# A two-layer hybrid decoder trunk on one core: the low part of every second weight unit made by an accumulating transfer

## The chip, the cores and the metric

The kernel runs on 1 core of one Trainium2 chip. The metric is the device time of one execution in microseconds. Three runs of the kernel before gave 2230.68, 2228.06 and 2229.37 us, a median of 2229.37 us.

## The reference

The program is a float32 trunk of two layers over 512 tokens of width 1024. Each layer has an adaLN-modulated RMS norm, a mixer with three parallel branches (retention, RG-LRU, mLSTM), then a second norm and a squared-ReLU MLP of width 4096. Cut to what matters:

```python
for l in range(2):
    mod = silu(c) @ w_ada[l] + b_ada[l]          # 6 x 1024 columns
    sh1, sc1, g1, sh2, sc2, g2 = split(mod, 6)
    h = rms_norm(x, norm_mix[l]) * (1 + sc1) + sh1
    proj = h @ w_in[l]                           # 1024 -> 8192
    ret, lru, mls = the three branches of proj
    merged = sum(sigmoid(gate_b) * (branch_b @ w_br_b[l]))
    x = x + g1 * (merged @ w_out[l])
    h = rms_norm(x, norm_mlp[l]) * (1 + sc2) + sh2
    x = x + g2 * (square(relu(h @ w_ff1[l])) @ w_ff2[l])
return rms_norm(x, final_norm)
```

Nearly all the arithmetic is in products with weights, and all of it is asked for in float32.

## The kernel before, in words

Activations lie with features on partitions and the 512 tokens along the free axis. A weight matrix is cut into units: a unit is 128x1024 float32 (512 KB), the weights of 128 output features for all 1024 input features. There are 352 units, 176 a layer, counted from 0 in the order of use (`plan_units`, L100).

TensorE multiplies in fp32r, a shortened float32. So every operand is split in two fp32r parts, a high part that ScalarE makes by a copy (L96) and a low part, the operand minus the high part (L97), and each product is three matmuls: high times high (L184), high times low (L185), low weights times high (L186). A unit is 8 such groups of three, 24 matmuls over 512 columns (`project`, L188, and `unit_products`, L198). In the retention's values the tokens are the stationary side, and the three matmuls stand on L923 to L925.

The weight stream is written out by hand. `next_w` (L154) moves the count of used units on and calls `w_ahead` (L141), which emits loads of raw units on SP's queue so that three are ahead of use, and splits so that two units are ready beyond the one in use. Three buffers hold raw units (`raw`), three the high parts (`wh`), three the low parts (`wl`). So the split of unit n can start when TensorE has finished unit n-3, and from then two units' products run before unit n is wanted. `split_next` (L149) makes one split: high part on ScalarE, low part on VectorE, or on GpSimd for the first five units (`split_engine`).

Three places use the buffers otherwise. `update_x` (L203) takes its last three units at once and runs them first over one half of the tokens, then over the other, so their buffers come free late. `first_units` (L230), which follows each inner norm, takes the next three at once in the same way. `ret_values` (L910) takes two at once. `update_x` followed by `first_units` comes three times: from mixer to MLP in both layers, and from the MLP of layer 0 to the mixer of layer 1.

The modulation is computed beside the products. `ada_unit` (L380) loads a 512 KB piece of `w_ada` into a `raw` buffer and VectorE multiplies it with the condition in two instructions. 80 such pieces are emitted one after each unit (`step`, L168) in the first two `merge` stages of layer 0 and in its MLP, so there weight units and modulation pieces share the three `raw` buffers and SP's queue.

The framework that compiles the kernel puts the instructions of each engine in order, chooses the buffers and writes the semaphores. GpSimd (POOL) has 155 small instructions and issues no transfers.

Of the kernel before, what the change touches and what calls it, by code (L numbers as in the profile page):

```python
# [9 lines left out]
F32 = mybir.dt.float32  # L10
# [3 lines left out]
ALU = mybir.AluOpType  # L14
# [11 lines left out]
# column offsets in the packed parameter array of a layer  # L26
# [5 lines left out]
# column offsets in the packed constants  # L32
# [3 lines left out]
# order in which the columns of the modulation are computed: (which of the six, k tile)  # L36
# [7 lines left out]
# causal score blocks: key tile -> (first query column, columns, offset in the packed scores)  # L44
# [3 lines left out]
# order of the mLSTM's input (m) and output gate (o) tiles, in the first layer and in the others  # L48
M_ORDER = ("mmmmmoommmoo", "mmmommommmoo")

# input projection tiles (of 128 columns) by part
# [3 lines left out]
class Trunk:  # L55
# [38 lines left out]
    def split(self, hi, lo, src, eng=None):  # L94
        """hi + lo == src exactly; both are float32r."""
        self.act(hi, src, AF.Copy)  # L96
        self.tt(lo, src, hi.bitcast(F32), ALU.subtract, eng)  # L97

# [50 lines left out]
    def split_next(self, wh, wl):  # L149
        self.split(wh, wl, self.raw.pop(self.n_split), self.split_engine)  # L150
        self.parts[self.n_split] = (wh, wl)
        self.n_split += 1

    def next_w(self, count=1):  # L154
        """The next weight units, with the ones after them on their way."""
        self.n_used += count
        self.w_ahead(3, 2)
        return self.take_w(count)
# [5 lines left out]
    def later(self, units, f):  # L164
        """Emit f after that many more units of products."""
# [22 lines left out]
    def project(self, hs):  # L188
        """The next unit's 128 output features (partitions) for all tokens."""
# [13 lines left out]
    def update_x(self, hs, gate, follow):  # L203
        """x += gate * (hs times the next eight units), and what follow makes of the new x.

        The last three units go through the first half of the tokens and then through the second,
        so that the norm of the first half passes behind the products of the second.
        follow(0) and follow(1) return what is to be emitted for TensorE a unit later."""
# [21 lines left out]
    def first_units(self, hs_half, late):  # L230
        """The next three units, for the first half of the tokens and then for the second.

        hs_half(h) yields the split tokens of a half, k tile by k tile; late() is emitted early on."""
# [16 lines left out]
    def total(self, ps, src, first=True, last=True):  # L250
        """Sum over partitions, on every partition, of a split src."""
# [5 lines left out]
    def setup(self):  # L257
# [29 lines left out]
        # silu of the condition  # L287
# [11 lines left out]
    def small_params(self):  # L299
        """Halved biases and 2 softplus(-lambda) of every layer, one column per feature tile."""  # L300
# [16 lines left out]
        # e = exp(-|lam|): powers of two split off, a polynomial for the rest  # L317
# [14 lines left out]
        # log(1 + e) = 2 atanh(e / (2 + e))  # L332
# [9 lines left out]
        # softplus(-lam) = max(-lam, 0) + 2 q  # L342
# [5 lines left out]
    def rotary_angles(self):  # L348
        """Position times frequency, brought into [-pi, pi]."""
# [30 lines left out]
    def ada_unit(self, l, c, i):  # L380
        """Products of two k tiles with a chunk of 512 modulation columns, summed over the k tiles."""
# [15 lines left out]
    def ada_load(self, l, c, tag="qk"):  # L397
        """The weights of a chunk of 512 modulation columns, a tile for each k tile."""
# [7 lines left out]
    def ada_mixed(self, raws, on_pe):  # L406
        """The sums of a chunk on every partition, the first on_pe k tiles on TensorE and the others on VectorE."""
# [17 lines left out]
    def ada_columns(self, l, i, ps):  # L425
        """Four column tiles of the modulation from their values along the free axis."""
# [28 lines left out]
    def square_sum(self, k, cols=ALL):  # L455
        """Running sum of squares of x[0..6]; x[7] is left apart."""
# [4 lines left out]
        if 0 < k < KT - 1:  # L461
            acc = self.sq_tiles[0][:, cols]
            self.tt(acc, acc, sq, ALU.add)
            if k == KT - 2:
                # has the table of the root loaded before the root is waited for
                self.act(sq[:, :1], sq[:, :1], AF.Sqrt)

    def row_scale(self, cols=ALL):
        """1 / sqrt(mean of squares + eps) per token, on every partition."""
# [22 lines left out]
    def modulated(self, l, second, late):  # L492
        """The normed and modulated tokens, split, and the products of the next three units."""
# [9 lines left out]
    def first_modulated(self):  # L503
        """As modulated, for the first layer, with the modulation itself and the first units' products."""
        count = 3
        # VectorE has the modulation to do
# [17 lines left out]
        # two more units, kept where nothing else is yet  # L524
# [25 lines left out]
    def gate_weights(self, l):  # L550
        """w_if applied after the block-diagonal q, k, v maps: one [1024, 8] map per input, split."""
# [12 lines left out]
        # the blocks of Wq Wk^T, of which the scores are made  # L564
# [6 lines left out]
        # the silu branch arrives doubled  # L571
# [8 lines left out]
    def conv(self, ps, cw, cb, j):  # L580
        """Causal depthwise convolution of a projected tile along the tokens."""
# [7 lines left out]
    def m_first(self, l, j, ps):  # L589
        """Convolution of one tile of the mLSTM input, and the input split for its gates."""  # L590
# [8 lines left out]
    def m_second(self, pg, first):  # L599
        """Twice the silu of the convolution, split for the gates."""  # L600
# [19 lines left out]
    def m_rows(self, l, pg):  # L620
        """Stabiliser rows of the four heads from the gate pre-activations."""
# [23 lines left out]
        # running maximum, split over partitions 0..3 and 32..35  # L645
# [6 lines left out]
        # 4 eps exp(-2 (F + max))  # L652
# [530 lines left out]
def lay_out(v):  # L1183
# [12 lines left out]
    o = {}  # L1196
# [71 lines left out]
```

## Time and profile before

| | |
|---|---|
| median of three runs | 2229.37 us |
| span of the profiled execution, first to last instruction | 2226.5 us |
| TensorE (PE) busy | 2180.9 us, 98% of the span |
| VectorE (DVE) busy | 1387.4 us, 62% |
| ScalarE (ACT) busy | 1037.8 us, 47% |
| GpSimd (POOL) busy | 171.9 us, 8% |
| moved by DMA | 248.93 MB, 112 GB/s on average |

The profiled execution has no time of its own beside its span; the median of the runs is 2.8 us above that span, which is taken as what lies around it. PE is the row of matmuls and PEld the row of weight loads that overlap them. Matmuls are pipelined: one shows as some 0.39 us and the next starts 0.23 us later, so busy time alone doesn't tell whether TensorE is fed; start times do.

### The profile page before, as it was taken

Reading aid. Unit: us, or ns where it says so; the run is one execution under the profiler, and the core shown is the slowest. Engines: PE = TensorE matmul, PEld = TensorE weight load, DVE = VectorE, ACT = ScalarE, POOL = GpSimd, SP = SyncE. Lnnn points to the kernel's source line nnn. Section 1 sums busy time; section 2 is a strip of 40 time slices with the busy share of each in tenths; the row PEclk is TensorE's granted clock in tenths of the full one; section 3 lists DMA queues with packets and bytes.
Section 4 is the critical chain, followed back from the end, with each engine's and each line's share of the span. In section 5 each row is a group of like instructions: output and inputs, shape, how many; then the busy total and the mean of one; then the engine's idle time right before and its main releaser. Section 6 shows DMA issues by size and latency. Waiting matters only on the chain.

```text
span 2226.5 us, 26615 instructions
## 1 busy us (share of the span) xinstructions
PE 2180.9 (98%) x10534; PEld 1817.5 (82%) x10534; DVE 1387.4 (62%) x1867; ACT 1037.8 (47%) x1474; POOL 171.9 (8%) x155
## 2 busy tenths in 40 slices
PE   5999999999999999999999999999999999999998
PEld 3778888888878888888897888888887889888887
DVE  7879766766774576666477872557547556333335
ACT  3566335562583353342446652455528525342342
POOL 2322001002100000000001210000111000000000
PEclk9999999999999999999999999999999999999999
DMA  8211552226423246656322123232322332322322
GB/s 288 74 46 46 171 176 81 96 91 211 129 74 114 86 150 194 188 189 190 125 83 89 34 72 102 84 97 78 107 95 81 95 100 88 96 94 99 100 95 67
DMA packets 75375, 248.93 MB, mean 112 GB/s; under 512 B 8561, under 2 KB 12273, under 8 KB 75249
## 3 DMA queue, kind: packets, MB, share of 16 engines
q1 hardware_dynamic: 75248, 247.23, 35.1%
q8 instruction: 82, 1.34, 0.2%
q14 instruction: 45, 0.36, 0.0%
HBM read 245.10 MB, written 2.10 MB: 111 GB/s over the span
## 4 chain that ended last, share of the span: by engine, by line
PE 85%; DVE 7%; ACT 5%; DMA 2%; issue 1%; SPq 0%; POOL 0%; DVEq 0%; ACTq 0%
PE acc L185 26%; PE acc L186 26%; PE acc L184 26%; PE acc L925 1%; PE acc L924 1%; PE acc L923 1%; ACT t L80 1%; DVE t L83 1%; DVE wl L86 1%; ACT L80 1%; ACT wh L80 1%; DVE qk L1033 1%; DMA big<-in_w_ada 1%; DVE sl L86 0%; PE acc L254 0%
## 5 line engine op out<-in xcount | busy, mean ns | idle before, releaser
L80 ACT ACTIVATE wh<-raw 128x1024 fp32r<-128x1024 f32 x350 | 370.4, 1059 | 834.4 <-PE acc L185 760.4
L185 PE MATMUL acc<-hl,wh 128*128 128x512 f32 (+1 forms) x1720 | 657.1, 383 | 1.5 <-DVE hl L83 1.5
L184 PE MATMUL acc<-hh,wh 128*128 128x512 f32 (+1 forms) x1720 | 655.6, 383 | 2.5 <-ACT hh L80 2.2
L186 PE MATMUL acc<-hh,wl 128*128 128x512 f32 (+1 forms) x1720 | 655.9, 382 | 0.9 <-DVE wl L86 0.9
L86 DVE TENSOR_TENSOR wl<-raw,wh 128x1024 fp32r<-128x1024 f32 x347 | 433.6, 1250 | 317.9 <-ACT wh L80 313.2
L184 PEld LDWEIGHTS acc<-hh,wh 128*128 128x128 f32 x1720 | 323.6, 189 | 71.1 <-ACT hh L80 4.0
L185 PEld LDWEIGHTS acc<-hl,wh 128*128 128x128 f32 x1720 | 324.7, 189 | 64.5 <-DVE hl L83 2.7
L186 PEld LDWEIGHTS acc<-hh,wl 128*128 128x128 f32 x1720 | 324.7, 189 | 64.5 <-DVE wl L86 1.5
L184 PE MATMUL acc<-big,wh 128*128 128x512 f32 (+1 forms) x944 | 357.5, 379 | 0.0
L186 PE MATMUL acc<-big,wl 128*128 128x512 f32 (+1 forms) x944 | 357.4, 379 | 0.0
L185 PE MATMUL acc<-big,wh 128*128 128x512 f32 (+1 forms) x944 | 357.3, 378 | 0.0
L186 PEld LDWEIGHTS acc<-big,wl 128*128 128x128 f32 x944 | 177.6, 188 | 33.7 <-DVE wl L86 0.7
L185 PEld LDWEIGHTS acc<-big,wh 128*128 128x128 f32 x944 | 177.6, 188 | 33.7 <-DVE big L86 0.3
L184 PEld LDWEIGHTS acc<-big,wh 128*128 128x128 f32 x944 | 177.6, 188 | 33.3
L83 DVE SCALAR_TENSOR_TENSOR ada<-raw,cond,ada 128x512 f32<-128x512 f32 x140 | 104.7, 748 | 61.2 <-DMA raw<-in_w_ada 59.5
L83 DVE SCALAR_TENSOR_TENSOR x<-acc,mod,x 128x512 f32<-128x512 f32 (+1 forms) x70 | 49.1, 702 | 126.1 <-PE acc L186 125.9
L80 ACT ACT_TABLE_LOAD x72 | 92.4, 1283 | 6.8 <-DVE t L83 4.9
L80 ACT ACTIVATE t<-t 128x512 f32<-128x512 f32 (+3 forms) x120 | 72.0, 600 | 19.6 <-DVE t L86 8.0
L924 PE MATMUL acc<-wl,hh 128*128 128x256 f32 x256 | 72.4, 283 | 0.0
L925 PE MATMUL acc<-wh,hl 128*128 128x256 f32 x256 | 72.4, 283 | 0.0
L923 PE MATMUL acc<-wh,hh 128*128 128x256 f32 x256 | 72.4, 283 | 0.0
L83 DVE SCALAR_TENSOR_TENSOR t<-acc,par,t 128x511 f32<-128x511 f32 (+2 forms) x96 | 70.1, 739 | 3.3 <-ACT t L80 3.0
(260 smaller groups left out, 2581.7 us busy)
## 6 DMA issues: line engine op xcount, KB each, us to landing
raw<-in_w_in SPq DMA_DIRECT2D x160, 512.0 KB, 3.5
raw<-in_w_ff SPq DMA_DIRECT2D x128, 512.0 KB, 3.5
raw<-in_w_ada SPq DMA_DIRECT2D x80, 512.0 KB, 3.5
raw<-in_w_br SPq DMA_DIRECT2D x48, 512.0 KB, 3.6
raw<-in_w_out SPq DMA_DIRECT2D x16, 512.0 KB, 3.5
qk<-in_w_ada SPq DMA_DIRECT2D x16, 256.0 KB, 5.3
big<-in_w_ada SPq DMA_DIRECT2D x16, 256.0 KB, 6.0
bd<-in_decay SPq DMA_DIRECT2D x8, 320.0 KB, 2.9
```

The costliest lines, as they stand in the source:

```text
L80: self.nc.scalar.activation(out, in_, f, **kw)
L83: self.nc.vector.scalar_tensor_tensor(out, a, s, b, op0=op0, op1=op1)
L86: (eng or self.nc.vector).tensor_tensor(out, a, b, op=op)
L184: mm(ps, lhsT=wh, rhs=xh, start=first, stop=False)
L185: mm(ps, lhsT=wh, rhs=xl, start=False, stop=False)
L186: mm(ps, lhsT=wl, rhs=xh, start=False, stop=last)
L923: mm(dst, lhsT=hh[:, tok], rhs=wh, start=kt == 0, stop=False)
L924: mm(dst, lhsT=hh[:, tok], rhs=wl, start=False, stop=False)
L925: mm(dst, lhsT=hl[:, tok], rhs=wh, start=False, stop=kt == KT - 1)
L1033: self.nc.vector.tensor_tensor_scan(ix, a, w, 0.0, op0=ALU.mult, op1=ALU.add)
```

## The change

In `split_next`, a unit with an odd number (and not among the first five, which have a `split_engine`) gets its low part in two steps: ScalarE writes the negated high part into `wl`, and a transfer issued from POOL's queue adds the raw unit onto it. All other units are split as before. The buffer that the framework keeps for descriptors of POOL's transfers grows from 1024 to 2048 bytes a partition.

```diff
     def split_next(self, wh, wl):
-        self.split(wh, wl, self.raw.pop(self.n_split), self.split_engine)
+        raw = self.raw.pop(self.n_split)
+        if self.n_split % 2 and self.split_engine is None:
+
+            self.act(wh, raw, AF.Copy)
+            self.act(wl, wh.bitcast(F32), AF.Copy, scale=-1.0)
+            self.nc.gpsimd.dma_start(wl.bitcast(F32), raw, accum_op=ALU.add)
+        else:
+            self.split(wh, wl, raw, self.split_engine)
         self.parts[self.n_split] = (wh, wl)
         self.n_split += 1
...
-    nc = bacc.Bacc("TRN2", target_bir_lowering=False, num_devices=1, dynamic_dma_scratch_size=1024)
+    nc = bacc.Bacc("TRN2", target_bir_lowering=False, num_devices=1, dynamic_dma_scratch_size=2048)
```

The rest of the diff removes comments and docstrings.

## Rows read from the trace of the kernel before

**Rows 1.** The page: busy time of the engines, and TensorE's in 40 slices.

```profile
PE 2180.9 (98%) x10534; PEld 1817.5 (82%) x10534; DVE 1387.4 (62%) x1867; ACT 1037.8 (47%) x1474; POOL 171.9 (8%) x155
PE   5999999999999999999999999999999999999998
```

**Rows 2.** The page's groups: the two halves of a split, busy and mean ns.

```profile
L80 ACT ACTIVATE wh<-raw 128x1024 fp32r<-128x1024 f32 x350 | 370.4, 1059 | 834.4 <-PE acc L185 760.4
L86 DVE TENSOR_TENSOR wl<-raw,wh 128x1024 fp32r<-128x1024 f32 x347 | 433.6, 1250 | 317.9 <-ACT wh L80 313.2
```

**Rows 3.** Waits of TensorE's weight loads that VectorE ended: total us, times, longest.

```profile
PEld acc L185 <- DVE xs L86: 5.2, 8, 0.9
PEld acc L185 <- DVE sl L86: 2.5, 4, 0.8
PEld acc L186 <- DVE wl L86: 2.2, 5, 0.5
```

**Rows 4.** Timeline, an ordinary unit of layer 1's MLP: start us, us, instruction [idle before].

```profile
1902.81 1.06 ACT L80 ACTIVATE wh<-raw 128x1024 fp32r<-128x1024 f32 x1 [2.56 <-PE acc L185]
1903.91 1.23 DVE L86 TENSOR_TENSOR wl<-raw,wh 128x1024 fp32r<-128x1024 f32 x1 [2.93 <-ACT wh L80]
...
1914.17 0.39 PE L186 MATMUL acc<-big,wl 128*128 128x512 f32 x1
```

**Rows 5.** Timeline, three odd units around layer 1's inner norm: split start, first low-part matmul.

```profile
1843.50 1.06 ACT L80 ACTIVATE wh<-raw 128x1024 fp32r<-128x1024 f32 x1 [4.00 <-PE acc L185]
1849.42 0.28 PE L186 MATMUL acc<-mg,wl 128*128 128x256 f32 x1
...
1858.69 1.06 ACT L80 ACTIVATE wh<-raw 128x1024 fp32r<-128x1024 f32 x1 [1.98 <-PE acc L185]
1862.48 0.28 PE L186 MATMUL acc<-hh,wl 128*128 128x256 f32 x1
...
1879.33 2.01 ACT L80 ACTIVATE wh<-raw 128x1024 fp32r<-128x1024 f32 x2 [2.75 <-PE acc L185]
1881.95 0.40 PE L186 MATMUL acc<-hh,wl 128*128 128x512 f32 x1
```

**Rows 6.** Timeline, the same pair for two odd units of the RG-LRU's part, layer 0.

```profile
488.67 1.05 ACT L80 ACTIVATE wh<-raw 128x1024 fp32r<-128x1024 f32 x1
494.83 0.39 PE L186 MATMUL acc<-hh,wl 128*128 128x512 f32 x1
...
666.35 1.06 ACT L80 ACTIVATE wh<-raw 128x1024 fp32r<-128x1024 f32 x1
673.27 0.39 PE L186 MATMUL acc<-hh,wl 128*128 128x512 f32 x1
```

**Rows 7.** DMA issues: queue, operation, count, KB each, median us from issue to landing.

```profile
raw<-in_w_ff SPq DMA_DIRECT2D x128, 512.0 KB, 3.5
raw<-in_w_ada SPq DMA_DIRECT2D x80, 512.0 KB, 3.5
...
gcols<-in_gcols SPq DMA_DIRECT2D x1, 8.0 KB, 1.6
```

**Rows 8.** Timeline of layer 0's MLP: two odd units' splits and the loads between.

```profile
897.61 1.06 ACT L80 ACTIVATE wh<-raw 128x1024 fp32r<-128x1024 f32 x1 [2.56 <-PE acc L185]
898.91 1.21 DVE L86 TENSOR_TENSOR wl<-raw,wh 128x1024 fp32r<-128x1024 f32 x1
900.16 0.33 SPq L138 DMA_DIRECT2D raw<-in_w_ff  x1
902.87 0.33 SPq L138 DMA_DIRECT2D raw<-in_w_ada  x1
...
909.35 1.04 ACT L80 ACTIVATE wh<-raw 128x1024 fp32r<-128x1024 f32 x1
```

**Rows 9.** Timeline of POOL: the same addition twice, in the second merge.

```profile
501.67 3.48 POOL L86 TENSOR_TENSOR mg<-mg,t 128x512 f32<-128x512 f32 x1 [5.86 <-DVE t L83]
512.36 1.30 POOL L86 TENSOR_TENSOR mg<-mg,t 128x512 f32<-128x512 f32 x1 [7.22 <-DVE t L83]
```

**Rows 10.** Stretches around the mLSTM's gate rows: us, busy us (instructions), granted clock, DMA share.

```profile
116.00:121.40 5.40, 3.23 (x12) 0.80 (x10) 3.09 (x4) 3.79 (x7) 1.73 (x2) 1.00 0.00 0
121.40:124.90 3.50, 3.50 (x8) 2.32 (x8) 1.26 (x3) 2.26 (x4) 0.00 (x0) 0.51 0.53 154
```

## The prediction

> **What bounds the kernel now.** I read the page's busy times first, then the waits of TensorE, then the timeline of single units. TensorE is at 9 tenths or more in every slice but the first and the last, 98% overall, and VectorE at 62% [rows 1]. So VectorE's load is not what sets the time. What it could give back is what TensorE waits for it: the longest such waits of the weight loads sum to 5.2 + 2.5 + 2.2 = 9.9 us in the whole run, and of these the subtraction that the change takes away accounts for 2.2 [rows 3]. That is the ceiling of a gain: some 10 us. The loss has no such ceiling, because the low part of a weight unit lies on a chain that ends at a matmul.
>
> That chain is read in the timeline. In an ordinary unit ScalarE starts the high part at 1902.81, as TensorE frees the buffer; VectorE's subtraction runs from 1903.91 to 1905.14; the first matmul that reads the low part starts at 1914.17 [rows 4]. I call the time from the first to the last of these the lead: 11.36 us, of which the split now takes 2.3 and 9.0 are spare. The lead is two units of products, and it's this that covers the change. It is not the same everywhere. Around a norm three units hold all three buffers to the end, and the odd units there have leads of 5.92, 3.79 and 2.62 us [rows 5]. In the RG-LRU's part ScalarE comes late to two odd units: 6.16 and 6.92 us [rows 6].
>
> **The change part by part.** It touches the odd units from 5 to 351, 174 of them.
>
> *Removed:* 174 subtractions of 1.25 us, 217 us of VectorE [rows 2]. As it isn't the bound, this is worth between nothing and the 9.9 us above; I take 3, the subtraction's own 2.2 and a little of the rest.
>
> *Added on ScalarE:* 174 passes of 1.06 us, 184 us [rows 2]. ScalarE is at 47% and mostly waits for TensorE before a split, so next to long leads this costs nothing; without that cover each would cost 1.06. Where it falls ahead of the normed tokens' pass at the three norms I count it: 3 us.
>
> *Added on POOL and the DMA engines:* 174 transfers of 512 KB. POOL's instruction waits for ScalarE's second pass, and POOL's own additions and masks queue behind it; POOL is at 8%, so I price that at nothing, at most a POOL instruction (1.3 to 3.5 us [rows 9]) for the few that a scan waits for. No row shows a transfer from POOL's queue, nor one that adds. The nearest are the plain loads: 512 KB lands 3.5 us after issue, 8 KB after 1.6 [rows 7]. So 1.6 is fixed and 1.9 is data. An adding transfer must read two operands for each byte written; I take the data part twice, 1.6 + 3.8 = 5.4 us. The bounds are 3.5 (an addition that costs nothing) and 7.3 (data part three times: two reads and a write), and above that whatever POOL's start adds. I take 5.4 as the plain load is the nearest row and the second operand is certain.
>
> The Trainium skill, "DMA: Bandwidth & Descriptors", section on the anatomy of a DMA on the gpsimd path, fits 2.0 us plus bytes at 436 GB/s for a transfer issued there, an estimate of 3.2 us here. By it the sum below would come to about 2238 us, the cheap case among the rivals. It is a fit for copies, and no run shown so far has one.
>
> So the chain of an odd unit becomes 1.06 + 1.06 + some 0.1 of hand-overs + 5.4 = 7.6 us, in place of 2.3. Against an ordinary lead of 11.36 it stays hidden, with 3.7 to spare. Against the short leads TensorE waits:
> - at each norm 7.6 - 5.9, 7.6 - 3.8 and 7.6 - 2.6: 1.7 + 3.8 + 5.0 = 10.5; three times: 31.5 us;
> - the last odd unit, like the first of these: 1.7;
> - two units at 6.16 and two at 6.92, one of each in either layer: 2 x 1.4 + 2 x 0.7 = 4.2.
>
> Together 37.4 us. These waits don't overlap, as each unit's buffer is freed after the one before has waited.
>
> *Moved:* the release of the raw buffer, from the end of the subtraction to the landing of the transfer. Where modulation pieces share the buffers, a unit's load is issued the moment the subtraction two units earlier ends (900.12, issue 900.16 [rows 8]). It lands 3.5 later, 5.7 us before ScalarE takes it up at 909.35. The release comes 7.6 instead of 2.5 us after the split's start, so the load comes 5.1 later and still lands 0.6 ahead. But SP's queue is in order, and the modulation piece issued at 902.87 stands behind it: 905.6 at the earliest, 2.7 later. VectorE gets 1.25 back in the same pair of units, so a pair falls behind by up to 1.5. There are 80 pieces [rows 7], so 40 pairs: 60 us, less the 9.0 us of slack [rows 4] that each of three stretches starts with, 33. The lower bound is 0, if the order on SP's queue adapts; I take the middle, 16.
>
> *The clock.* After 5.4 us in which TensorE was busy 3.23, the next 3.5 us ran at a granted clock of 0.51, so near 1.2 GHz, else 2.4 [rows 10]. Six of the stalls above are 3.8 us or more. If each is followed by such a stretch, it loses half of 3.5, together 10; I take half of that, 5.
>
> **Sum:** 37.4 + 16 + 5 + 3 - 3 = 58. On the profiled span of 2226.5 that is 2284.5; with the 2.8 us around it (the median of the runs is 2229.4) it gives about **2288 us**.
>
> **The rivals.**
>
> *A slower transfer.* If the data part is three times that of a load, the chain is 9.5: 16.2 us at each norm, 49 in all, some 30 at the other leads under 9.5 (by the same two start times of every odd unit), and where modulation pieces run, the load comes 1.3 us too late in each of 40 pairs, 52 more. About +142: 2371 us. For it: no row shows an addition on the way. Against it: nothing either.
>
> *POOL held up by VectorE.* The same addition on POOL takes 1.30 or 3.48 us [rows 9], so POOL is slowed by something beside it, and VectorE is busy 62% of the time. If that holds for issuing too and adds about a VectorE instruction, 1.2 us, the chain is 8.8: 62 us at short leads, some 40 among the modulation pieces, 6 for the clock: 2337 us. The Trainium skill, "SBUF — State Buffer", section on the two sides of SBUF, says that GpSimd can't write descriptors while VectorE holds their shared port, in a fast mode above all; by it this is the case to expect, and the trace shows POOL's spread, not yet a transfer.
>
> *A cheap transfer.* At 3.5 us the chain is 5.7: 1.9 + 3.1 at each norm, 15 in all, nothing elsewhere, less up to 6 for VectorE: about 2238 us.
>
> *Faster.* Every transfer lands within 1.6 us, the fixed part alone, because its data stay on the chip. The chain is 3.8, only the third unit of a norm waits (3 x 1.2), and VectorE's relief shortens the waits behind it by their full 9.9: 2223 us. It decides where the transfer takes under some 2.4 us. Against it: even 8 KB took 1.6 [rows 7].
>
> *The change doesn't do what it says*, the framework ordering the transfers so that TensorE's order changes: no reason in the rows.
>
> **How the numbers follow.** The forecast, a transfer of 4 to 6.5 us, has 0.53; the slower transfer 0.15; POOL held up 0.12; the cheap one 0.12, of which about half would be within 0.2%; faster 0.05; not as it says 0.03, taken as no difference. A measurement of this kernel can tell some 0.2%, 4.5 us, from no change. So slower by more has 0.53 + 0.15 + 0.12 + 0.06 = 0.86, the same 0.09, faster 0.05. The range reaches from the cheap case, 2238, to a little above the slower one, 2390; below it lie the fastest cases, above it both slow mechanisms together.
>
> **What would show it.** The group of VectorE's subtractions falls to about 173, the passes of ScalarE on a unit rise by 174, and a queue of POOL's appears with some 91 MB. Right: its landing takes 5 to 6 us from issue; the longest waits of TensorE for a transfer into `wl` stand at the three norms, near 4 and 5 us; ordinary units of layer 1's MLP keep their rhythm. Wrong: waits for `wl` in ordinary units of that MLP (the transfer takes over 9 us), or none at the norms (under 1.6). If SP's queue shows the modulation pieces in their old rhythm, the 16 us are wrong; if no stretch of low clock follows the norms, the 5 are.

## The result and the profile after

The changed kernel takes **2340.9 us** (median of four runs, 2339.6 to 2341.8), the kernel before 2229.2; the ratio is 1.0498, with a 95% interval from 1.0483 to 1.0513. That is 112 us more, where the forecast said 58 more.

The page of the changed kernel: busy times, POOL's queue, the chain that ended last, the groups of the three steps of a split, and the DMA issues. Its line numbers are 7 higher than those of the kernel before (L193 was L186).

```profile
PE 2216.0 (95%) x10534; PEld 1831.5 (78%) x10534; DVE 1181.9 (51%) x1693; ACT 1204.9 (51%) x1648; POOL 312.7 (13%) x329
...
q0 software_dynamic: 25056, 91.24, 21.0%
...
PE 45%; issue 21%; DMA 17%; DVE 10%; ACT 6%; POOL 1%; SPq 0%; POOLq 0%; DVEq 0%; ACTq 0%
...
L155 POOL DMA_DIRECT2D wl<-raw x174 | 151.1, 869 | 1481.0 <-ACT wl L80 1250.6
L86 DVE TENSOR_TENSOR wl<-raw,wh 128x1024 fp32r<-128x1024 f32 x173 | 215.0, 1243 | 220.5 <-ACT wh L80 218.0
L80 ACT ACTIVATE wl<-wh 128x1024 fp32r<-128x1024 f32 x174 | 183.6, 1055 | 2.8
...
wl<-raw POOLq DMA_DIRECT2D x174, 512.0 KB, 4.6
...
raw<-in_w_ff SPq DMA_DIRECT2D x128, 512.0 KB, 4.1
raw<-in_w_ada SPq DMA_DIRECT2D x80, 512.0 KB, 4.1
```

The change did what it says: 173 subtractions are left of 347 [rows 2], ScalarE has 174 more passes, and POOL's queue moves 91 MB. VectorE fell from 62% to 51% [rows 1] and TensorE with it, from 98% to 95%, and now a DMA is in the chain for 17% of the span. The plain loads land later too, at 4.1 us where it was 3.5 [rows 7].

The waits of the changed kernel (total us, times, longest): two of TensorE, one of ScalarE and one of VectorE.

```profile
PE acc L193 <- DMA wl<-raw: 43.6, 24, 4.1
...
PE acc L931 <- DMA wl<-raw: 10.7, 6, 2.0
...
ACT wh L80 <- DMA raw<-in_w_ff: 98.8, 24, 6.4
...
DVE ada L83 <- DMA raw<-in_w_ada: 167.6, 56, 6.1
```

TensorE waits for a transfer only 30 times, 54 us in all, so half of the loss isn't there. The other half shows one step earlier: ScalarE's *first* pass now waits for the load of a unit of the MLP, 24 times, which it did not do once in the kernel before. Weight units come late, and with them both halves of the split. (ScalarE's 98.8 us are idle time, not yet a loss of TensorE's.)

**Where the time went.** From the start of the first low-part matmul of one stage to that of the next, in TensorE's timeline of both kernels, I took each stage's length in the profiled execution; the table gives how much longer it is than in the kernel before (the first column says where in that kernel's span it begins; the last row is the difference of the spans). Modulation pieces run in the three stages with a star. The other columns belong to the experiments below (e11 has none).

```
stage (begins at, us)              after    e1    e2    e3    e4    e5    e6    e7    e8    e9   e10   e12
start (0)                           -1.0   1.3  -0.4   1.2   0.2   0.3   0.5  -0.2   0.1  -1.8   1.1   0.1
mLSTM, layer 0 (76.9)                5.9   6.7   6.1   4.8   3.5   5.5   3.3   2.7   1.2   1.5   3.4   0.1
* first merge (229.0)               11.6   0.0   0.0  13.4   0.0   0.0  13.7   0.0  11.4   0.0   8.2   5.1
retention heads (319.5)              7.7   5.8   6.0   5.0   1.8  16.8  11.7   0.0   2.7   0.0   7.4   3.8
* RG-LRU, second merge (453.5)      15.1  -0.3   5.4  14.3   5.9  11.6   8.7  -0.3   1.8   5.6  14.6  12.0
gates, branch, output (643.4)        1.3   1.8   5.0   1.8   0.1   0.2   2.1   0.1   0.1   0.0   0.1   0.0
inner norm, layer 0 (760.9)          8.4   6.8   6.6   8.0   4.2   0.8  13.3   0.0   1.0   0.0   7.6   0.0
* MLP, layer 0 (809.6)              32.0   0.2  -0.2  32.1   5.8  10.5  55.8  -0.2  56.1  16.8  27.4  28.2
outer norm (1120.1)                  8.2   8.3   6.5   8.2   2.5   0.8  15.0   0.0   0.0   0.0   5.5   0.0
mLSTM, first merge, l. 1 (1169.9)    1.2   0.2   1.4   1.5   0.2   4.7   0.3   0.8   0.9   0.0   1.0   0.0
retention heads (1405.4)             5.9   5.8   6.0   4.9   1.0  17.4  13.1   0.0   2.5   0.0   7.5   0.0
RG-LRU to output, l. 1 (1539.0)      7.1   6.8   7.0   3.6   6.7  11.6   9.5   0.0  -0.1   0.0   0.0   0.0
inner norm, layer 1 (1843.7)         8.3   8.2   8.3   6.6   4.4   0.8  12.0   0.4   1.6   0.0   5.5   0.0
MLP, layer 1 (1892.4)                0.0   0.0   0.0   0.0   0.0   0.0   0.0   0.1   0.1   0.0   0.0   0.0
last three units (2196.8)            1.8   1.6   1.8   1.9   0.2  -0.3   2.7   0.1   0.1  -0.1   1.0   0.1
span                               113.6  53.1  59.6 107.2  36.6  80.9 161.8   3.6  79.7  22.0  90.2  49.4
```

Layer 1's MLP, 304 us with 28 transfers and the long leads of [rows 4], costs nothing. The starred stages cost 58.7 us, the three norms 24.9, the retention heads 13.6, the RG-LRU's part and what follows it outside the starred stages 8.4, the mLSTM of layer 0 with the start 4.9; the mLSTM of layer 1 and the last three units make up the other 3.0.

**The loop beside the modulation pieces.** The changed kernel's timelines of POOL, SP and ScalarE in layer 0's MLP, put in order of time (the columns are those of [rows 8]).

```profile
905.30 0.33 SPq L138 DMA_DIRECT2D raw<-in_w_ff  x1
...
908.87 1.06 ACT L80 ACTIVATE wh<-raw 128x1024 fp32r<-128x1024 f32 x1 [4.92 <-DMA raw<-in_w_ff]
...
911.38 0.87 POOL L155 DMA_DIRECT2D wl<-raw  x1 [10.54 <-ACT wl L80]
...
916.87 0.33 SPq L138 DMA_DIRECT2D raw<-in_w_ff  x1
...
929.67 0.33 SPq L138 DMA_DIRECT2D raw<-in_w_ff  x1
```

The load of an odd unit is issued at 905.30 and ends ScalarE's 4.92 us of waiting at 908.87; the transfer starts at 911.38; and the moment it has landed, at 916.87, the raw buffer is taken for the load of the odd unit after it. This turn takes 11.6 us, the next one, to the load at 929.67, 12.8. Two units of products take 48 matmuls: the stretches below show how long that is. They count the matmuls that started in 200 us of layer 0's MLP, first of the kernel before, then of the changed one (us, PE, PEld, DVE, ACT, POOL, granted clock, DMA share, GB/s).

```profile
870.00:1070.00 200.00, 200.00 (x882) 165.12 (x881) 134.16 (x186) 76.49 (x102) 0.00 (x0) 1.00 0.61 190
```

```profile
880.00:1080.00 200.00, 187.27 (x787) 151.61 (x785) 100.08 (x152) 81.74 (x104) 13.85 (x16) 0.96 0.74 209
```

Before, 48 matmuls took 200 x 48 / 882 = 10.9 us, less than either turn; after, they take 200 x 48 / 787 = 12.2, the mean of the two turns. So here the loop of the raw buffer, not TensorE, sets the time, and no lead however long would hide it.

**A norm.** The changed kernel's timeline around layer 1's inner norm: ScalarE's split of each of the three odd units of [rows 5], and the matmul that waits for its transfer.

```profile
1946.92 1.06 ACT L80 ACTIVATE wh<-raw 128x1024 fp32r<-128x1024 f32 x1 [3.95 <-PE acc L192]
...
1954.44 0.38 PE L193 MATMUL acc<-mg,wl 128*128 128x256 f32 x1 [1.39 <-DMA wl<-raw]
...
1963.81 1.06 ACT L80 ACTIVATE wh<-raw 128x1024 fp32r<-128x1024 f32 x1 [1.98 <-PE acc L192]
...
1971.06 0.39 PE L193 MATMUL acc<-hh,wl 128*128 128x256 f32 x1 [1.15 <-DMA wl<-raw]
...
1985.52 2.01 ACT L80 ACTIVATE wh<-raw 128x1024 fp32r<-128x1024 f32 x2 [4.72 <-PE acc L192]
...
1988.84 0.50 PE L193 MATMUL acc<-hh,wl 128*128 128x512 f32 x1 [0.53 <-DVE wl L86]
...
1995.43 0.50 PE L193 MATMUL acc<-hh,wl 128*128 128x512 f32 x1 [2.89 <-DMA wl<-raw]
```

The chains are 7.5, 7.3 and 9.9 us long, but TensorE waits only 1.39, 1.15 and 2.89, together 5.4: the matmul at 1988.84 is already one of the unit *after* the third odd unit. Five k tiles of that unit (five groups of three matmuls) now stand ahead of the waiting matmul in TensorE's order, which the framework chose. The third chain is long because its transfer, issued at 1988.83, lands some 6.6 us later, where the median is 4.6; why, the trace doesn't show.

### The profile page after: what moved, and what is told of

It reads as the page before. It is cut to its first block, busy times and chain, and to the rows that moved or that the text cites. A ratio compares the mean times of both kernels' runs of the same rounds, so it can differ in the third digit from the quotient of the medians.

```text
span 2340.1 us, 27227 instructions
## 1 busy us (share of the span) xinstructions
PE 2216.0 (95%) x10534; PEld 1831.5 (78%) x10534; DVE 1181.9 (51%) x1693; ACT 1204.9 (51%) x1648; POOL 312.7 (13%) x329
## 4 chain that ended last, share of the span: by engine, by line
PE 45%; issue 21%; DMA 17%; DVE 10%; ACT 6%; POOL 1%; SPq 0%; POOLq 0%; DVEq 0%; ACTq 0%
PE acc L192 14%; PE acc L193 14%; PE acc L191 14%; DMA raw<-in_w_ada 7%; DMA wl<-raw 6%; DVE ada L83 2%; DMA raw<-in_w_ff 2%; ACT t L80 2%; ACT wh L80 1%; PE acc L931 1%; PE acc L932 1%; PE acc L930 1%; DVE wl L86 1%; ACT L80 1%; DVE t L83 1%
## 5 line engine op out<-in xcount | busy, mean ns | idle before, releaser
L193 PE MATMUL acc<-hh,wl 128*128 128x512 f32 (+1 forms) x1720 | 664.2, 387 | 35.7 <-DMA wl<-raw 34.1
L191 PE MATMUL acc<-hh,wh 128*128 128x512 f32 (+1 forms) x1720 | 663.5, 387 | 2.2 <-ACT hh L80 1.6
L193 PEld LDWEIGHTS acc<-hh,wl 128*128 128x128 f32 x1720 | 328.1, 191 | 108.3 <-DMA wl<-raw 42.0
L193 PE MATMUL acc<-big,wl 128*128 128x512 f32 (+1 forms) x944 | 360.8, 382 | 13.9 <-DVE wl L86 7.1
L155 POOL DMA_DIRECT2D wl<-raw x174 | 151.1, 869 | 1481.0 <-ACT wl L80 1250.6
L86 DVE TENSOR_TENSOR wl<-raw,wh 128x1024 fp32r<-128x1024 f32 x173 | 215.0, 1243 | 220.5 <-ACT wh L80 218.0
L193 PEld LDWEIGHTS acc<-big,wl 128*128 128x128 f32 x944 | 179.2, 190 | 49.3 <-DMA wl<-raw 8.0
L80 ACT ACTIVATE wl<-wh 128x1024 fp32r<-128x1024 f32 x174 | 183.6, 1055 | 2.8
L86 DVE TENSOR_TENSOR big<-t,big 128x512 fp32r<-128x512 f32 x72 | 53.1, 738 | 110.4 <-ACT big L80 110.4
```

The source lines that it names most:

```text
L80: self.nc.scalar.activation(out, in_, f, **kw)
L86: (eng or self.nc.vector).tensor_tensor(out, a, b, op=op)
L155: self.nc.gpsimd.dma_start(wl.bitcast(F32), raw, accum_op=ALU.add)
L191: mm(ps, lhsT=wh, rhs=xh, start=first, stop=False)
L193: mm(ps, lhsT=wl, rhs=xh, start=False, stop=last)
```

## The experiments

Each edit is a diff against the changed kernel; the numbers of a run by stage stand in its column of the table above.

### e1: no adding transfer beside the pieces

```diff
-        if self.n_split % 2 and self.split_engine is None:
+        if self.n_split % 2 and self.split_engine is None and not (self.fill_every and self.filler):
```

> The adding transfer is left out only while modulation pieces run (some 40 of the 174 odd units go back to VectorE's subtraction). Theory: those units cost most because they share three raw buffers and SP's queue with the pieces, and TensorE's starts there fell behind by some 56 us in all; without them 2341 - 56 = 2285 us, and VectorE's wait for a modulation piece (167.6 us after, 59.5 before) goes back to about 60. Rival: all adding transfers cost alike, 112 / 174 = 0.64 us each, through traffic on the DMA engines: 2341 - 40 x 0.64 = 2315 us.

Measured: 2281.9 us, ratio 1.0239 [1.0223, 1.0254]. The starred stages lose nothing (0.0, -0.3, 0.2), all others about what they lose in the changed kernel. With 40 of the 174 transfers gone, half of the loss is gone; that all cost alike is out.

### e2: a buffer of their own for the pieces

```diff
-        raw = self.load_raw(self.t["w_ada"][l, c, i])
+        raw = self.tile([P, KT * P], F32, self.piece_tag, 1)
+        self.nc.sync.dma_start(raw, self.t["w_ada"][l, c, i])
...
+        self.piece_tag = "sh" if first else "vh"
```

> All 174 adding transfers stay; the modulation pieces get one buffer of their own, so the weight units keep all three raw buffers. Theory: the loss beside the pieces is one of buffers (a raw buffer is held until its transfer has landed, and the piece and the next unit wait for it), so most of the 56 us go: about 2285 us, at most 2300. Rival: the loss is one of traffic (unit loads, pieces and transfers on the same DMA engines at once), or of VectorE's time for the pieces: the time stays at 2330 to 2345 us, with landings of 5 to 7 us in these stretches.

Measured: 2290.9 us, 1.0277 [1.0261, 1.0292]. All 174 transfers stay, and the first merge and the MLP lose nothing. Here is the same 200 us of its MLP, and the DMA issues of that stretch:

```profile
880.00:1080.00 200.00, 200.00 (x883) 165.40 (x882) 116.60 (x171) 87.81 (x111) 15.55 (x18) 1.00 0.82 237
```

```profile
raw<-in_w_ff SPq DMA_DIRECT2D x37, 512.0 KB, 4.7
...
wl<-raw POOLq DMA_DIRECT2D x18, 512.0 KB, 4.6
```

TensorE has its 883 matmuls back with the DMA engines at 0.82, busier than in any other run, and with loads that land at 4.7 us. So neither traffic nor late loads harm in this stretch, where a unit's load has three buffers to itself. The second merge still loses 5.4 us, and the gates after it lose 5.0, more than the 1.3 of the changed kernel; why, was not followed up.

### e3: a higher priority for the second pass

```diff
-            self.act(wl, wh.bitcast(F32), AF.Copy, scale=-1.0)
-            self.nc.gpsimd.dma_start(wl.bitcast(F32), raw, accum_op=ALU.add)
+            with self.tc.high_priority(400):
+                self.act(wl, wh.bitcast(F32), AF.Copy, scale=-1.0)
+                self.nc.gpsimd.dma_start(wl.bitcast(F32), raw, accum_op=ALU.add)
```

> The second pass of ScalarE and the transfer get a higher priority, so that the pass follows the first one at once. Theory: in the six places where a retention head's values are made, and in part elsewhere, the transfer started late as other ScalarE work stood between the two passes (in one of them 3.2 us), which cost 13.6 us there; that goes to about 0, and 5 to 15 us more in the merges: 2312 to 2328 us, and in those six places no wait for wl of over 1 us. Rival: the work that stood between is itself waited for, and its delay takes the place of the wait: 2335 to 2345 us.

Measured: 2334.5 us, 1.0472 [1.0444, 1.0501]: the expectation failed. The changed kernel's timeline of ScalarE and POOL, and TensorE's wait, at a retention head's values shows what was to be moved:

```profile
1515.60 1.06 ACT L80 ACTIVATE wh<-raw 128x1024 fp32r<-128x1024 f32 x1 [2.58 <-PE acc L192]
1516.68 1.28 ACT L80 ACT_TABLE_LOAD   x1
1517.97 0.69 ACT L80 ACTIVATE t<-acc,eps 128x512 f32<-128x512 f32 x1
1518.68 1.20 ACT L80 ACTIVATE t<-acc 64x512 f32<-64x512 f32 x2
1519.90 1.06 ACT L80 ACTIVATE wl<-wh 128x1024 fp32r<-128x1024 f32 x1
...
1521.33 0.89 POOL L155 DMA_DIRECT2D wl<-raw  x1
...
1525.94 0.38 PE L931 MATMUL acc<-wl,hh 128*128 128x256 f32 x1 [1.71 <-DMA wl<-raw]
```

A table load, a root and two copies, 3.2 us, stand between the two passes, and the chain is 10.3 us. With the priority only the two copies moved behind the pass, the table load and the root stayed, and the six places went from 13.6 to 9.9 us. The step is right as far as it went; it is small.

### e4: the transfer without the addition

The low part of an odd unit is the raw unit itself here.

```diff
-            self.nc.gpsimd.dma_start(wl.bitcast(F32), raw, accum_op=ALU.add)
+            self.nc.gpsimd.dma_start(wl.bitcast(F32), raw)
```

> The transfer copies the raw unit onto the low part's buffer without adding, so the low part of an odd unit is the raw unit itself. Theory: the addition costs about 1.1 us of the 4.6 from issue to landing; the copy lands at 3.5, as a plain load does, and each of the some 24 longest waits and the loop beside the modulation pieces shorten by that: about 2341 - 35 = 2306 us. Rival: the 4.6 us are the price of POOL's queue (its start and both ends on the chip), not of the addition: landing 4.4 to 4.6, time 2335 to 2345 us.

Measured: 2266.5 us, 1.0166 [1.0151, 1.0181]; from its page, the queue, the group on POOL and the issue:

```profile
q0 software_dynamic: 25056, 91.24, 10.0%
...
L155 POOL DMA_DIRECT2D wl<-raw x174 | 94.9, 545 | 1458.5 <-ACT wl L80 1291.8
...
wl<-raw POOLq DMA_DIRECT2D x174, 512.0 KB, 2.9
```

The addition costs 1.7 of the 4.6 us, and two thirds of the 112 us hang on that. On the DMA engines a copy takes 10.0% of 2263 us, 226 us, over 174 transfers: 1.30 us of the 16 engines' time each. With the addition it is 21.0% of 2340 us over 174: 2.82. So an adding transfer is 2.2 copies for the engines, and POOL needs 0.87 us to issue it, not 0.55. The Trainium skill, "DMA: Bandwidth & Descriptors", section on the anatomy of a DMA on the gpsimd path, estimates 3.2 us for a copy of this size: the trace agrees within 0.3 (2.9), and the addition is outside of that fit.

### e5: the extra pass, with the addition on VectorE

```diff
-            self.nc.gpsimd.dma_start(wl.bitcast(F32), raw, accum_op=ALU.add)
+            self.tt(wl, raw, wl.bitcast(F32), ALU.add)
```

> ScalarE's negation pass stays on the 174 odd units, and VectorE adds the raw unit onto it (no transfer), so only the extra pass is priced. Theory: nearly all of the 112 us is the transfer's latency and what it holds; the pass makes the chain 2.3 + 1.1 = 3.4 to 3.6 us, which only the third unit of each norm (lead 2.63) and late passes at the retention values feel: 3 to 10 us over the kernel before, 2232 to 2239 us. Rival: ScalarE's 184 us more of work in its queue cost as much as the transfer (passes behind table loads and evictions, clock stalls): 2260 us or more.

Measured: 2305.6 us, 1.0343 [1.0329, 1.0357]: 76 us over the kernel before, with no transfer at all. That is some 67 us beyond the theory and inside the rival's range. TensorE's wait in the six places where a retention head's values are made, and, from the timelines of ScalarE and VectorE at one of them, the second pass and the addition:

```profile
PE acc L931 <- DVE wl L86: 21.8, 6, 3.6
```

```profile
1480.73 1.06 ACT L80 ACTIVATE wl<-wh 128x1024 fp32r<-128x1024 f32 x1
...
1488.02 1.21 DVE L86 TENSOR_TENSOR wl<-raw,wl 128x1024 fp32r<-128x1024 f32 x1
```

The second pass comes late here as in the changed kernel, and the addition starts another 6.2 us after it has ended (1481.79 to 1488.02), behind VectorE's work for the head. TensorE waits 21.8 us for it in the six places; the retention heads lose 34 us, where the changed kernel loses 13.6. At the norms, where the second pass follows soon, it is 0.8 each. So the transfer has one merit here: it takes the late pass up on a queue with little else. The extra pass is not cheap by itself; it depends on what stands ahead of it and of the step that takes it up. The 76 us and the 112 are different losses in different stages and don't add up.

### e6: the raw unit from HBM

```diff
-            self.nc.gpsimd.dma_start(wl.bitcast(F32), raw, accum_op=ALU.add)
+            self.nc.gpsimd.dma_start(wl, self.units[self.n_split].bitcast(F32R), accum_op=ALU.add)
```

> The adding transfer takes the weight unit from HBM a second time, not from the raw buffer, so the raw buffer is free after ScalarE's first pass; all 174 stay. Theory: beside the modulation pieces it was the raw buffer, held until the transfer had landed, that cost some 56 us; that goes, and the waits at norms and retention values (short leads) stay: 2280 to 2292 us, as with a piece buffer of its own. Rival: the 91 MB read a second time meet the loads on the DMA engines, landings go to 6 us and more, and the waits at the short leads grow: 2310 to 2345 us.

Measured: 2386.9 us, 1.0691 [1.0669, 1.0713], beyond both. The stretch in the MLP and its issues:

```profile
880.00:1080.00 200.00, 176.31 (x728) 142.63 (x727) 94.49 (x141) 73.96 (x95) 13.75 (x16) 0.94 0.71 194
```

```profile
raw<-in_w_ff SPq DMA_DIRECT2D x30, 512.0 KB, 4.6
wl<-in_w_ff POOLq DMA_DIRECT2D x16, 512.0 KB, 7.4
```

The raw buffer is free after ScalarE's first pass, and yet the starred stages lose 78 us instead of 59. The adding transfer from HBM lands at 7.4 us beside the loads, and those of units at 4.6. So a loss of this size also comes without a held buffer, here with a slower transfer; how much of the changed kernel's loss the held buffer makes, this run can't tell, and a run for each half followed (e9, e12).

### e7: only the long leads

```diff
-        if self.n_split % 2 and self.split_engine is None:
+        if self.n_split % 2 and self.split_engine is None and self.n_split not in SHORT_LEADS and not (self.fill_every and self.filler):
```

`SHORT_LEADS` names 28 odd units with leads under 9 us, or near the start; 108 transfers are left.

> Adding transfers only where the lead in the kernel before was 9 us or more and no modulation piece runs, some 110 units; VectorE subtracts for the others. Theory: a hidden transfer costs nothing, and VectorE's relief there is worth nothing either, as TensorE doesn't wait for it there: 2226 to 2233 us, within 0.2% of the kernel before. Rival: each transfer costs something whatever the lead (traffic, ScalarE's queue, clock), 0.2 us or more: 2250 us or more.

Measured: 2231.9 us, 1.0010 [1.0001, 1.0019]. 108 hidden transfers cost some 2 us together, and the 135 us of VectorE that they save (108 x 1.25) give nothing back.

### e8: the long leads, from HBM, beside the pieces too

e7's list with e6's transfer.

> As the run before it, with the transfer taken from HBM, and used beside the modulation pieces too, where the raw buffer now comes free 1.2 us earlier than in the kernel before. Theory: layer 0's stages beside the pieces are some 9 us slower than layer 1's in the kernel before, and an earlier release of the raw buffer and VectorE's relief take back part of it: 2219 to 2227 us, a gain of 2 to 10 us. Rival: those stages wait for VectorE's own work on the pieces or for the traffic, which the second read raises: 2230 to 2245 us.

Measured: 2306.0 us, 1.0341 [1.0327, 1.0355]: no gain, but 69 us lost in the starred stages alone, and beyond both ranges. Two waits of TensorE and one of VectorE point to two ways:

```profile
PE acc L197 <- DMA wl<-in_w_ff: 19.6, 7, 5.3
PE acc L196 <- DVE big L90: 19.3, 6, 5.9
```

```profile
DVE ada L87 <- DMA raw<-in_w_ada: 188.6, 57, 7.6
```

In seven places the transfer from HBM comes late even to units that had leads of 9 us and more in the kernel before. And a piece lands late, VectorE waits for it, and the activations (`big`) behind that in VectorE's queue come late to TensorE. Which of the two weighs more, this run doesn't show.

### e9: the buffer held, nothing moved

```diff
...
+            self.split(wh, wl, raw, self.split_engine)
+            hold = self.tile([P, 4], F32, "hold", 1)
+            self.act(hold, wh.bitcast(F32)[:, :4], AF.Copy)
+            for _ in range(2):
+                self.nc.gpsimd.dma_start(hold, raw[:, :4], accum_op=ALU.add)
```

This stands for the odd units beside pieces; all others are split as before.

> VectorE subtracts everywhere as in the kernel before; for the odd units beside modulation pieces two tiny transfers of 2 KB, one after the other, read the raw buffer after ScalarE's pass, so the raw buffer is held about as long as by the adding transfer (4 to 6 us past the pass), but no 512 KB are moved and no chain reaches TensorE. Theory: the held raw buffer alone makes the loads late beside the pieces: 30 to 55 us over the kernel before, 2260 to 2285 us. Rival: the loss there needs the traffic of the large transfer, or the chain to the matmul: 2229 to 2240 us.

Measured: 2251.3 us, 1.0096 [1.0082, 1.0109], between the two. From the timelines of ScalarE and SP, how long the buffer is held, and the stretch in the MLP:

```profile
899.99 1.06 ACT L80 ACTIVATE wh<-raw 128x1024 fp32r<-128x1024 f32 x1 [5.67 <-DMA raw<-in_w_ff]
...
907.48 0.33 SPq L138 DMA_DIRECT2D raw<-in_w_ff  x1
```

```profile
870.00:1070.00 200.00, 192.72 (x829) 156.87 (x828) 123.34 (x178) 70.67 (x108) 29.23 (x34) 0.98 0.59 179
```

Held for 7.5 us from the split's start in this turn, where the changed kernel holds it for 8.0 (908.87 to 916.87; over the MLP the median is 8.0 in both), the buffer alone costs 5.6 + 16.8 = 22.4 us of the 58.7, with a DMA share even under that of the kernel before.

### e10: the negated part first

```diff
-            self.act(wh, raw, AF.Copy)
-            self.act(wl, wh.bitcast(F32), AF.Copy, scale=-1.0)
+            self.act(wl, raw, AF.Copy, scale=-1.0)
             self.nc.gpsimd.dma_start(wl.bitcast(F32), raw, accum_op=ALU.add)
+            self.act(wh, raw, AF.Copy)
```

> On an odd unit ScalarE makes the negated high part first, straight from the raw unit, then the transfer starts, and the high part comes after; all 174 stay. Theory: the transfer starts one pass (1.06 us) earlier everywhere, and 3 to 4 us earlier where other ScalarE work stands between the two passes: the retention values lose nearly nothing (13.6 us gained), each norm some 2, the stages beside the pieces 5 to 15: 2341 - 30 = 2311 us, between 2300 and 2320. Rival: the high part, now second, is what TensorE and the framework's order wait for instead: 2330 us or more.

Measured: 2318.4 us, 1.0397 [1.0383, 1.0412], the size expected, but not from the places expected. The norms, the starred stages and layer 1's RG-LRU gain; the retention values don't (14.9 us instead of 13.6). There the framework still runs the high part first:

```profile
1501.41 1.06 ACT L80 ACTIVATE wh<-raw 128x1024 fp32r<-128x1024 f32 x1 [2.58 <-PE acc L192]
1505.72 1.06 ACT L80 ACTIVATE wl<-raw 128x1024 fp32r<-128x1024 f32 x1
```

That the retention values lose nothing once the pass is early is therefore not shown: neither this edit nor e3 made it early there.

### e11: the pieces' buffer alone

The kernel before with e2's edit.

> The kernel before with one buffer of their own for the modulation pieces, and no adding transfer. Theory: three shared buffers bring loads just in time in the kernel before too (layer 0's stages beside the pieces are some 9 us slower than layer 1's), and weight units with all three buffers for themselves gain a few of these: 2222 to 2227 us. Rival: the 9 us are VectorE's and TensorE's work on the pieces, not their buffers: 2228 to 2231 us.

Measured: 2229.3 us, 0.9999 [0.9990, 1.0007]. No gain: in the kernel before the three shared buffers are enough, and the rival's range holds.

### e12: the whole transfer, read by nobody

```diff
...
+            self.split(wh, wl, raw, self.split_engine)
+            spare = self.tile([P, KT * P], F32, self.piece_tag, 1)
+            self.act(spare, wh.bitcast(F32), AF.Copy, scale=-1.0)
+            self.nc.gpsimd.dma_start(spare, raw, accum_op=ALU.add)
...
```

Again for the odd units beside pieces alone.

> VectorE subtracts everywhere, so TensorE waits for no transfer. For the odd units beside modulation pieces ScalarE's negation pass and the full adding transfer run too, into a spare buffer that nothing reads: the raw buffer is held and 512 KB are moved as in the changed kernel. Holding alone cost 22 us (2251). Theory: the transfer's traffic makes the loads of units and pieces later still, and holding and traffic together are most of the some 56 us lost beside the pieces: 2270 to 2285 us, loads and pieces landing at about 4.1 us. Rival: the traffic costs nothing, and what holding leaves is the chain to the matmul, which is cut here: 2248 to 2258 us.

Measured: 2276.9 us, 1.0216 [1.0202, 1.0230], as the theory had it. Its stretch in the MLP, and ScalarE's wait for late units:

```profile
880.00:1080.00 200.00, 188.16 (x791) 151.40 (x790) 117.60 (x170) 82.71 (x104) 13.82 (x16) 0.96 0.76 212
```

```profile
ACT wh L80 <- DMA raw<-in_w_ff: 105.1, 28, 6.8
```

791 matmuls, as good as the 787 of the changed kernel, though TensorE waits for no transfer: in the MLP 28.2 of the 32.0 us are there without any chain to a matmul. In the three starred stages it is 45.3 of 58.7. By these runs holding makes some 22 of the 59, and the large transfer with its extra pass on top of it 23; the rest, 13, is left for the chain to the matmul. How the 23 divide is not shown: this run holds the buffer as long as e9 in the median turn of the MLP (7.9 us), but in four of 21 turns its second pass comes 3.6 to 4.1 us after the first, and traffic alone did no harm in e2.

## Why the prediction came out as it did

The chain is the one forecast, hidden behind long leads and paid for at short ones; what it costs beside the pieces came about another way. The time lies in the stated range, but the loss is nearly twice the 58 us of the sum.

**Right: the chain.** Its parts were 1.06 + 1.06 + 0.1 + 5.4 = 7.6; the norm's first unit shows 7.5. The hand-over is some 0.4 (1519.90 + 1.06 to 1521.33) and the transfer 4.6, so the errors cancel in part. That the addition doubles the data part was sound: 2.82 us of the engines' time against 1.30. The dearer and the cheap transfer are out, as the usual case, and so is POOL held up by VectorE: each of the 174 issues takes POOL 0.85 to 1.04 us, and the norm's third chain, 9.9, is long in the landing (6.6), not in the issue. That rival's 2337 us lies next to the result by accident; its mechanism isn't there. The Trainium skill, "SBUF — State Buffer", section on the two sides of SBUF, keeps GpSimd from writing descriptors while VectorE runs an instruction in a fast mode that takes the shared port; that a busy VectorE makes this the case to expect was the forecast's own step, and no run here shows it. (The terms given for the slower transfer, 49, 30 and 52, sum to 131, not to its 142.)

**Signs that came out otherwise.** A landing of 5 to 6 us was foretold, the median is 4.6. The longest waits were to stand at the norms, near 4 and 5 us; at the norms the longest are 2.9 to 3.1, and the longest of all, 4.1 and 3.5, stand at the ends of layer 0's first merge and MLP, beside the pieces.

**Right: ordinary leads hide it.** Layer 1's MLP kept its rhythm to 0.0 us, and e7 shows the same for 108 units.

**Too large: the norms.** 31.5 us of waits were forecast; the one shown has 5.4, not 10.5, as the framework moves other products ahead. "No reason in the rows" for a change of TensorE's order was wrong. With the clock, the stage loses 8.2 to 8.4. The last odd unit, 1.7, measured 1.8.

**The step that failed: modulation pieces, 16 us forecast, 58.7 measured.** The rate came out near: "up to 1.5" a pair of units, times 40 pairs, 60 us; measured are 12.2 - 10.9 = 1.3 in the MLP. That is luck in part, as the way to it was another: the piece's load (issued at 908.46) goes out when VectorE is done with the piece before it, and doesn't stand behind a late load of a unit. "Still lands 0.6 ahead" rests on two odd units whose splits start 11.74 us apart (897.61 and 909.35 [rows 8]); at the mean of 10.9 the same chain is 0.2 late in every turn. Then I took off 9.0 us of spare time for each of three stretches, which is what an odd unit has over after the *old* split (11.36 - 2.3). After the new chain it has 11.36 - 7.6 = 3.7, and e12 shows that most of the loss doesn't come by way of the chain at all: the load is late for ScalarE, and both parts of the unit with it. And I took the middle between 33 and a lower bound of 0, "if the order on SP's queue adapts"; the load's place in the queue can't help when its buffer isn't free. What was missing is the closed loop, load plus chain until the buffer is free again, held against two units of products: 3.5 + 7.6 = 11.1 over the 10.9, and 11.6 to 12.8 in the two turns shown.

**Not in the forecast: the retention values, 13.6 us.** At the head shown under e3 the lead is some 8.6 us (the chain of 10.3 less the wait of 1.71), enough for the forecast's 7.6 with the passes back to back. But in ScalarE's order 3.2 us of other work come first there. That the extra passes cost nothing "next to long leads" and 3 us at the norms left out what they stand behind. That the late pass causes this loss is the trace's reading, which e3 bears out by 3.7 us; it is not shown for all of it.

**Undersized: the RG-LRU's part, 4.2 us.** It lost 8.4 with the gates and the output, 7.1 of them in layer 1, and e10, with the negated part first, takes these 7.1 away whole. There too the second pass comes late, 3.4 us after the first has ended (1671.08 to 1674.51), and the transfer goes out at 1677.18, behind two additions of POOL's. The longest wait of TensorE there:

```profile
1681.81 0.50 PE L193 MATMUL acc<-big,wl 128*128 128x512 f32 x1 [3.57 <-DVE wl L86]
```

The profile puts it down to VectorE's subtraction of another unit, which ended at 1681.75; the odd unit's transfer landed at 1681.72, so which of the two held the matmul isn't shown.

**POOL's queue, priced at nothing.** In layer 0's second merge five transfers go out 2.4 to 4.3 us after their second pass has ended, each behind an addition of POOL's (the addition at 553.30, the transfer at 554.98). What this costs by itself no run shows; it is part of the 15.1 us of that stage.

**The clock, 5 us: as priced at a norm, not foreseen elsewhere.** A stretch of the changed kernel with the stall after layer 1's inner norm, and what follows it (the columns are those of [rows 10]).

```profile
1993.20:1996.60 3.40, 1.17 (x5) 0.99 (x6) 1.17 (x2) 1.73 (x3) 0.86 (x1) 1.00 0.56 105
1996.60:2000.00 3.40, 3.40 (x10) 2.65 (x9) 0.00 (x0) 0.00 (x0) 0.00 (x0) 0.51 1.04 247
```

After 3.4 us in which TensorE was busy 1.17, the next 3.4 run at 0.51, near 1.2 GHz in place of 2.4: 1.7 us lost, as priced. What was not foreseen is that the pieces' stages do it too: in the 200 us of layer 0's MLP above the mean is 0.96, before it was 1.00. The mean granted clock of the span is 0.982, before it was 0.995: over 2340 us that is 42 us of full clock missing against 11, so at most 31 more, part of them while TensorE had nothing to do. This is inside the stages' losses above and not to be added to them.

**VectorE's gain, 3 us:** none (e7).

Altogether 58 forecast against 112: norms, clock and ScalarE's 3 us there 39.5 against 24.9, the last unit 1.7 against 1.8, pieces 16 against 58.7, RG-LRU 4.2 against 8.4, retention 0 against 13.6, layer 0's mLSTM with the start 0 against 4.9, layer 1's mLSTM 0 against 1.2, and 3 taken off for VectorE that didn't come. What makes the 4.9 and the 1.2 was not followed up. No run beat the kernel before: the best, e11 and e7, are level with it. A fourth raw buffer for the weight units was not tried.

## What to carry to other kernels

A step that frees a buffer later isn't priced by the lead of what it feeds, but by the loop of that buffer: load, all steps until it is free, next load, against the time that the consumer takes for as much. Where the loop is longer, every turn pays, and no lead saves it; here one more buffer for the pieces did, in two of three stages (e2). And work put on a second engine is only as early as the queues let it be, that engine's own and that of the engine which takes the work up: in e5 a late pass and an addition that came another 6.2 us later cost the retention heads more than the slow transfer did.

## What the runs showed of the hardware that was not expected

- An adding transfer of 512 KB within the chip takes 4.6 us from issue to landing, a copy 2.9; on the DMA engines 2.82 against 1.30 us, on POOL 0.87 against 0.55.
- From HBM the same addition lands 5.7 to 5.9 us after issue over the whole run and 7.4 beside the pieces' and units' loads of layer 0's MLP (e6).
- A transfer of 2 KB with an addition still takes 2.8 us from its issue to landing in the MLP of e9:

```profile
hold<-raw POOLq DMA_DIRECT2D x34, 2.0 KB, 2.8
```

- 0.82 of the DMA engines' time in use over 200 us did TensorE no harm where loads had buffers enough (e2); at 0.59, where they hadn't, it lost time all the same (e9).
